# Reordering the second-level Strassen products, moving one pair of sums from GpSimd to VectorE, and storing early blocks from GpSimd

## Chip, cores, metric

One core of one Trainium2 chip. The metric is the device time of one execution in microseconds (us).

## The reference, cut to what matters

```python
# x (16, 512, 768), w1 (768, 3072), b1 (3072), w2 (3072, 768), all float32
y = np.matmul(x, w1) + b1
y = 0.5 * y * (1.0 + erf(y / np.sqrt(2.0)))
return np.matmul(y, w2)
```

## The kernel before

The 8192 rows go through in eight blocks of 1024. Each block has a *first product* (x times w1, then GELU) and a *second product* (times w2). Both use the Strassen-Winograd scheme: seven products of half-sized matrices and some sums instead of eight products. In blocks 0 and 1 the second product has one level (four *units* of 128 rows). From block 2 on it has two levels: seven outer products (here also called *units*, in the order `ORDER`), each made of seven inner products (1 to 7), each of them 12 matmuls of 192 columns, about 0.99 us. The sums that make the operands and the outputs run on VectorE, some copies on ScalarE.

Two neighbouring units are interleaved so that TensorE has something to do while sums are made:

```python
ORDER = (1, 6, 7, 5, 2, 4, 3)          # outer products, in time
# period of unit i (j is the unit before it); fill(s) records side work
p1(i); copy_xy(i)      # bX -> bY by ScalarE
p7(j)                  # adds onto bY of j: bZ must have been made from it before
fill(1); p5(i); fill(2); p3(j); fill(3)
p6(i)                  # then VectorE: bZ = bY + quarter of an earlier output
fill(4); p4(j); fill(5); p2(i); fill(6)
```

So the addition after product 6 (`bZ<-bY`) has the three products p4, p2, p1 of time, about 3 us, before product 7 of the same unit needs it done. It stands in VectorE's queue among much other work. (A *slot* is one of the six calls of `fill`; the *turn* is the stretch where the last unit of one product is interleaved with the first unit of the next.)

The seven outer products share four output buffers `par[0..3]`. Unit 5 ends a part of the sums:

```python
add, dst = {1: (None, 0), 6: (0, 1), 2: (0, 0), 7: (1, 2), 5: (None, 3),
            3: (1, 1), 4: (2, 2)}[self.p]       # which par is added, which is written
...
if self.p == 5:                                  # in finish()
    for r in range(2):                           # "row sums", VectorE
        tt(par[1][:, r], par[1][:, r], self.dst[:, r], ADD)
    for r in range(2):                           # "bottom right sums", GpSimd
        nc.gpsimd.tensor_tensor(out=self.dst[:, r], in0=par[2][:, r],
                                in1=self.dst[:, r], op=ADD)
        self.store(r)
```

Blocks 0 and 1 have one output buffer, `osb`, stored from the sync queue:

```python
def right_done(self):
    nc.sync.dma_start(out=orr[...], in_=self.o[:, 0, :])
# in the second product of blocks 0 and 1, unit 1:
load_next_x(sb + 1, range(3, 6))                 # GpSimd's queue
for n in range(4):
    load_wt((sb + 1) * NH + n)                   # for block 2: sync queue, 672 KB each
# in block 1, from slot 2 on, units 0 to 2 and once more in unit 3: one sum on VectorE and its w2s copies to DRAM
```

Of the kernel before, what the change touches and what calls it, by code (L numbers as in the profile page):

```python
# [8 lines left out]
FP32 = mybir.dt.float32  # L9
F16 = mybir.dt.float16  # L10
P = 128
ADD = mybir.AluOpType.add
# [20 lines left out]
def kernel(  # L33
# [8 lines left out]
    nc = tc.nc  # L42
# [5 lines left out]
    RH = SB // 2  # L48
    nsb = R // SB
    KQ = K // P // 2  # L50
    NH = H // P // 2
    N2 = N // 2
    NU = RH // P
# [28 lines left out]
    ONE = 2  # L82
# [10 lines left out]
    def cut(off, n, pattern=None, **dims):  # L93
        ap = arena[:, off:off + n]
        return ap.rearrange(pattern, **dims) if pattern else ap
# [4 lines left out]
           for b in range(2)]  # L100
# [2 lines left out]
        "p (r t h n) -> p r t h n", r=2, t=2, h=2) for k in range(4)]  # L103
    tmps = [cut(o_par + 3 * k * PAR, 4 * RH).bitcast(FP32).rearrange("p (a r) -> p a r", a=2)
            for k in range(2)]
    stage = [cut(o_par + k * PAR + d * WB, WB, "p (c n) -> p c n", c=NQ)
             for k in (0, 3) for d in range(2)]
    assert 14 * NH * N4 + 2 * NH * P <= o_par
# [13 lines left out]
    with tc.manual_schedule():  # L122
# [3 lines left out]
        def tt(o, a, b, op):  # L126
            nc.vector.tensor_tensor(out=o, in0=a, in1=b, op=op)  # L127

        def later(n, f, q=None):
            (queue if q is None else q).append((70 + n * 0.52, f))  # L130

        def sums(ns):

            for q in (soon, queue):
                while q and ns >= q[0][0] * 0.6:
                    ns -= q[0][0]
                    q.pop(0)[1]()

        def flush(q):
            while q:  # L140
                q.pop(0)[1]()
# [80 lines left out]
            op(3, 4, b21, t[2], None)  # L222


        ORDER = (1, 6, 7, 5, 2, 4, 3)
        w2_order = [(ORDER[0], q) for q in (1, 2, 5, 6)]
        for i in range(1, 8):
            for d, q in ((0, 1), (1, 7), (0, 5), (1, 3), (0, 6), (1, 4), (0, 2)):
# [61 lines left out]
        def half_sums(c, ks=(0, 1, 2)):  # L290

            g11, g21, g22 = G1[:, c, 0, :], G1[:, c, 1, :], G2[:, c, 1, :]
            n = len(range(NH)[c]) * RH
            for k in ks:
                o, a, b, op = ((GA[:, c, :], g21, g22, ADD), (GB[:, c, :], GA[:, c, :], g11, SUB),
                               (g21, g11, g21, SUB))[k]
                later(n, lambda o=o, a=a, b=b, op=op: tt(o, a, b, op))

        def s4_sum(r, h):

            c, rr = slice(h * NQ, (h + 1) * NQ), slice(r * 2 * P, (r + 1) * 2 * P)
            later(NQ * 2 * P, lambda: tt(GB[:, c, rr], G2[:, c, 0, rr], GB[:, c, rr], SUB))
# [4 lines left out]
        def lev_sums(i, c0=0, c1=NQ, ks=(0, 1, 2, 3), q=None):  # L307

            A = OPERAND[ORDER[i]]
            a11, a12 = A[:, c0:c1, 0:2 * P], A[:, NQ + c0:NQ + c1, 0:2 * P]  # L310
            a21, a22 = A[:, c0:c1, 2 * P:RH], A[:, NQ + c0:NQ + c1, 2 * P:RH]
            s = [t[:, c0:c1, :] for t in lev_of(i)]
            for k in ks:
                a, b, op = ((a21, a22, ADD), (s[0], a11, SUB), (a11, a21, SUB),
                            (a12, s[1], SUB))[k]
                later((c1 - c0) * 2 * P, lambda k=k, a=a, b=b, op=op: tt(s[k], a, b, op), q)


        class Unit1:
# [2 lines left out]
            C = KQ  # L322

            def __init__(self, g, sb, k):
                self.g, self.sb = g, sb
                self.hi = hi_of(sb * NH + k)
                self.wt = wts[sb * NH + k]

# [7 lines left out]
                                     stop=c == self.C - 1, skip_group_check=True)  # L336

            def alloc(self):
                self.tmp = tmps[self.g % 2]

            def c12(self):
                return self.tmp[:, 0, :]
# [14 lines left out]
        class Unit2:  # L357
# [25 lines left out]
                return self.o[:, 1, N2:N]  # L383

            def right_done(self):
                nc.sync.dma_start(out=orr[:, self.sb * 8 + self.u, :], in_=self.o[:, 0, :])

            def left_done(self, row, bank):
                nc.scalar.copy(out=self.o[:, row, 0:N2], in_=bank[:, 0:N2])
                if row == 1:  # L390
                    nc.sync.dma_start(out=orr[:, self.sb * 8 + NU + self.u, :],
                                      in_=self.o[:, 1, :])

        class Unit3:

# [6 lines left out]
            def __init__(self, g, sb, i):  # L402
                self.g, self.sb, self.i = g, sb, i
                self.p = ORDER[i]
                add, dst = {1: (None, 0), 6: (0, 1), 2: (0, 0), 7: (1, 2), 5: (None, 3),
                            3: (1, 1), 4: (2, 2)}[self.p]
                self.add = None if add is None else par[add]
                self.dst = par[dst]
                self.alloc = lambda: None
# [50 lines left out]
            def finish(self):  # L460
                if self.p in (2, 3, 4):
                    self.store(0)
                    self.store(1)
                if self.p == 5:
                    for r in range(2):
                        tt(par[1][:, r], par[1][:, r], self.dst[:, r], ADD)
                    for r in range(2):
                        nc.gpsimd.tensor_tensor(out=self.dst[:, r], in0=par[2][:, r],  # L468
                                                in1=self.dst[:, r], op=ADD)
                        self.store(r)  # L470

        def p1(u, c0, c1):
            u.mm(1, bX[u.g % 2], True, c0, c1)
# [141 lines left out]

        def fill_mm1(sb, k, slot):
            n = sb * NH + k
            if slot == 1:
                if sb < ONE:
                    if k in (5, 9):  # L620
                        for s in range(4):
                            g_sum(s, 0, k - 5, k - 1)
                    if k == NH - 1:
                        for s in range(4):
                            g_sum(s, 0, 8, 10)
                    if sb == 0 and k in (4, 6, 8, 10):
                        prep_w2(*w2_parts[(k - 4) // 2])
                elif k in (6, 10):
                    lev_sums(0, *((0, 3) if k == 6 else (3, 5)), q=soon)
                elif k >= 3 and k % 2 == 1:  # L630
                    m = (k - 3) // 2
                    half_sums(slice(m, m + NQ + 1, NQ), (0, 1, 2) if m < 4 else (0, 1))
                    if k == 9:
                        lev_sums(1, 0, 3)
                        lev_sums(2, 0, 3)
                if k + 1 < NH:
                    prep_wt(n + 1)
                sums(900)
            if slot == 4:
                sums(1500)  # L640
            if slot == 3 and sb >= ONE and sb + 1 < nsb:
                if 1 <= k < 9:
                    load_x(sb + 1, k - 1)
                if 3 <= k < 11:
                    transpose_dma(sb + 1, k - 3)
            if slot == 5:
                if k + 3 < NH and (k >= 1 or sb > 0) and n + 3 not in wts:
                    load_wt(n + 3)
                if sb == 0:
                    for part in w2_loads[:2]:  # L650
                        load_w2(*part)
                    del w2_loads[:2]
                if sb >= ONE and k >= 3:
                    for m in range(2 * (k - 3), min(2 * (k - 2), RING)):
                        load_ring(sb, m)
            if slot == 6:
                flush(soon)
                if k == NH - 1 and sb < ONE:
                    flush(queue)
# [46 lines left out]
        def fill_mm2_two(sb, k, slot):  # L706
            if k == 0:
                if slot == 1:
                    lev_sums(0, NQ - 1, NQ, (0, 1), soon)
                    flush(soon)  # L710
                    lev_sums(0, NQ - 1, NQ, (2, 3), soon)
                    half_sums(slice(NQ - 1, NQ), (0, 1))
                    lev_sums(1, 3, NQ - 1)
                if slot == 6:
                    half_sums(slice(NH - 1, NH), (0, 1))
                    lev_sums(1, NQ - 1, NQ)
                    flush(queue)
                    for m in (NQ - 2, NQ - 1):
                        half_sums(slice(m, m + NQ + 1, NQ), (2,))
                    lev_sums(2, 3, NQ)  # L720
            elif slot == 1:
                if k == 3:
                    s4_sum(1, 1)
                if k in (2, 3, 4, 5):
                    lev_sums(k + 1)
                if k == 2:
                    s4_sum(0, 1)
            if k == 1 and slot == 4:
                s4_sum(1, 0)
                s4_sum(0, 0)  # L730
            if k > 0 or slot > 1:
                sums(1200)
            if slot == 6 and k > 0:
                flush(queue)
            if sb + 1 < nsb:
                if k in (0, 5, 6) and slot == 6:
                    load_wt((sb + 1) * NH + max(k - 4, 0))
                if k == 6 and slot == 1:
                    prep_wt((sb + 1) * NH)
                    x_sums(sb + 1, queue)  # L740
# [42 lines left out]
```

## Time and profile before

| | before |
|---|---|
| median of the runs (3) | 905.48 us (901.74 to 907.42) |
| span of the profiled run | 906.2 us |
| TensorE busy | 95% |
| second product of a two-level block, blocks 2 to 6, first matmul to the next block's first | 50.45 us each |
| second product of block 1 | 56.95 us |

The top of the page of the kernel before (busy time, share of the span, number of instructions):

```profile
span 906.2 us, 16269 instructions
...
PE 860.2 (95%) x6276; PEld 560.6 (62%) x6276; DVE 666.9 (74%) x1151; ACT 417.5 (46%) x680; POOL 148.1 (16%) x194
...
```

TensorE (PE) is the engine that bounds the kernel, so its idle time is the place to look. (DVE is VectorE, ACT ScalarE, POOL GpSimd; SPq is the sync engine, which here issues DMAs. bX, bY, bZ and bW are buffers in PSUM; arena and G lie in SBUF.) The waits of TensorE, longest in total first (engine, what it wrote, its line, what released it: us in total, times, longest):

```profile
PE bY L423 <- DVE bZ L516: 13.3, 12, 1.8
PE bY L334 <- DVE bZ L521: 7.3, 7, 3.2
PE bY L372 <- ACT bY L476: 5.1, 1, 5.1
...
```

The first line is the two-level blocks: twelve waits, two in each of six blocks, for the `bZ<-bY` addition. One of each pair is 0.5 us, the other 1.8. The longer one in block 2, in TensorE's timeline (start, duration, group, count, then the idle time before it and its releaser):

```profile
355.18 1.15 PE L423 MATMUL bX<-arena 128*128 128x192 f16 x12
358.09 1.15 PE L423 MATMUL bY<-arena 128*128 128x192 f16 x12 [1.75 <-DVE bZ L516]
```

Twelve matmuls start 0.99 us after the twelve before them when nothing is in the way; here it is 2.91, so 1.92 us are lost. VectorE and GpSimd in the time before:

```profile
351.68 1.64 DVE L127 TENSOR_TENSOR arena<-arena 128x1536 f16<-128x1536 f16 x1
...
353.71 2.52 DVE L127 TENSOR_TENSOR arena<-arena 128x1536 f16<-128x1536 f16 x1
...
356.61 0.94 DVE L127 TENSOR_TENSOR arena<-arena 128x1536 f16<-128x1536 f16 x1
357.48 0.55 DVE L516 TENSOR_TENSOR bZ<-bY,arena 128x384 f32<-128x384 f32 x1
```

```profile
350.10 2.40 POOL L468 TENSOR_TENSOR arena<-arena 128x768 f32<-128x768 f32 x1 [47.32 <-DVE arena L127]
353.58 1.82 POOL L468 TENSOR_TENSOR arena<-arena 128x768 f32<-128x768 f32 x1
```

VectorE never rests here. Two operations of one and the same shape (128x1536) take 1.64 and 2.52 us, the next 0.94. The long ones are those that run beside GpSimd's two sums. The bZ addition at 357.48 stands behind them all, and TensorE behind it.

Block 1 has the other large wait. ScalarE, TensorE and the sync queue there:

```profile
231.58 0.48 ACT L389 COPY arena<-bX 128x384 f32<-128x384 f32 x1 [13.39 <-DMA out_dram<-arena]
231.95 0.49 ACT L476 COPY bY<-bX 128x384 f32<-128x384 f32 x1
```

```profile
232.49 3.79 PE L372 MATMUL bY<-arena 128*128 128x384 f16 x12 [5.07 <-ACT bY L476]
236.11 2.11 PE L372 MATMUL bY<-arena,G 128*128 128x384 f16 x12
```

```profile
219.14 0.34 SPq L386 DMA_DIRECT2D out_dram<-arena  x1
```

A store issued at 219.14 lands only at about 231.5. ScalarE's copy into that buffer waits for it for 13.4 us; the copy TensorE needs stands behind. And then twelve matmuls take 3.79 us where the next twelve take 2.11: after an idle time of 5.1 us they start at half the rate. The Trainium skill, "TensorE: Matmul & The Clock Gate", section "What's actually happening", says that the array's clock is halved after an idle window of about 3.4 us. The trace agrees on the half rate (0.320 us from matmul to matmul instead of 0.163). After the waits of 1.8 us in the two-level blocks none was slow.

### The profile page before, as it was taken

The numbers are of one execution on the slowest core, as the hardware profiler recorded it, in microseconds if no ns is written. First come the engines' busy times: TensorE is split into PE (matmuls) and PEld (weight loads), VectorE is DVE, ScalarE is ACT, GpSimd is POOL, SyncE is SP. The second block draws the span as 40 slices with busy tenths as digits, with TensorE's granted clock in tenths as the row PEclk, the third lists the DMA queues.
The fourth block names the chain that finished last, engine by engine and source line by source line (L and its number), as shares of the span: only waits on it lengthen the run. The fifth ranks groups of instructions, "written<-read, shape, count | busy, mean of one in ns | idle before, by whom it ended". The sixth has DMA issues, their size and how long they took to land.

```text
span 906.2 us, 16269 instructions
## 1 busy us (share of the span) xinstructions
PE 860.2 (95%) x6276; PEld 560.6 (62%) x6276; DVE 666.9 (74%) x1151; ACT 417.5 (46%) x680; POOL 148.1 (16%) x194
## 2 busy tenths in 40 slices
PE   6989999989799999999999999999999999999995
PEld 2434654446454499546984479644996469844795
DVE  3688665645456699558995699767996689947995
ACT  2665116750147721576117751377215762177520
POOL 5553002400000003210041001300032000300013
PEclk8999999999999999999999999999999999999998
DMA  9999989949969789997999969997899969966495
GB/s 154 119 187 152 208 288 202 225 110 289 334 176 247 221 283 315 274 302 178 305 346 242 301 202 297 311 273 217 277 306 286 291 186 317 341 206 223 147 291 213
DMA packets 176525, 222.96 MB, mean 246 GB/s; under 512 B 106944, under 2 KB 115904, under 8 KB 176448
## 3 DMA queue, kind: packets, MB, share of 16 engines
q1 hardware_dynamic: 111680, 176.31, 62.2%
q0 software_dynamic: 64768, 45.62, 29.3%
q8 instruction: 49, 0.80, 0.3%
q14 instruction: 28, 0.23, 0.1%
HBM read 189.74 MB, written 47.87 MB: 262 GB/s over the span
## 4 chain that ended last, share of the span: by engine, by line
PE 67%; DVE 14%; DMA 10%; issue 4%; POOL 2%; ACT 2%; SPq 0%; POOLq 0%; DVEq 0%; ACTq 0%
PE bY L334 17%; PE bX L334 11%; PE bY L423 8%; DVE arena L127 7%; PE bW L334 5%; PE bZ L334 5%; PE bY L372 5%; PE bX L423 5%; DMA wt<-in_w_dram 4%; DMA wt<-w1s 4%; PE bX L372 3%; PE bW L423 3%; PE bZ L423 3%; DMA out_dram<-arena 1%; PE bZ L372 1%
## 5 line engine op out<-in xcount | busy, mean ns | idle before, releaser
L334 PEld LDWEIGHTS <-wt 128*128 128x128 f16 x2016 | 197.1, 98 | 250.9 <-issue 19.6
L423 PEld LDWEIGHTS <-arena 128*128 128x128 f16 x2664 | 221.2, 98 | 20.8 <-issue 15.1
L483 DVE TENSOR_TENSOR arena<-bY,pw 128x512 f32<-128x512 f32 (+1 forms) x104 | 70.8, 680 | 153.9 <-PE bY L334 98.7
L334 PE MATMUL bY<-XT,wt 128*128 128x512 f16 x576 | 155.8, 379 | 7.5 <-DVE bZ L521 7.3
L334 PE MATMUL bX<-XT,wt 128*128 128x512 f16 x576 | 143.0, 381 | 1.6 <-DMA wt<-w1s 1.5
L476 ACT COPY bY<-bX 128x512 f32<-128x512 f32 (+1 forms) x146 | 80.4, 551 | 131.9 <-DVE arena L455 105.0
L349 ACT ACTIVATE G<-arena,b1t 128x1024 f16<-128x1024 f32 x96 | 110.3, 1149 | 64.3 <-DVE arena L506 64.3
L127 DVE TENSOR_TENSOR arena<-arena 128x1536 f16<-128x1536 f16 (+5 forms) x176 | 129.7, 758 | 10.7 <-DMA w2s<-arena 9.8
L423 PE MATMUL bY<-arena 128*128 128x192 f16 x1224 | 115.6, 246 | 13.3 <-DVE bZ L516 13.3
L493 ACT COPY pw<-bW 128x512 f32<-128x512 f32 (+1 forms) x146 | 80.8, 554 | 83.0 <-PE bW L423 44.6
L334 PE MATMUL bW<-XS,wt 128*128 128x512 f16 x288 | 78.7, 383 | 4.0 <-DVE wt L127 4.0
L506 DVE TENSOR_TENSOR arena<-bZ,pw 128x512 f32<-128x512 f32 (+1 forms) x104 | 70.4, 677 | 15.9 <-PE bZ L334 14.0
L334 PE MATMUL bY<-XS,wt 128*128 128x512 f16 x288 | 79.1, 384 | 1.0 <-DVE wt L127 0.4
L468 POOL TENSOR_TENSOR arena<-arena 128x768 f32<-128x768 f32 x12 | 25.3, 2107 | 328.6 <-DVE arena L127 242.8
L334 PE MATMUL bZ<-XS,wt 128*128 128x512 f16 x288 | 78.5, 382 | 0.0
L248 POOL DMA_DIRECT2D xh<-in_x_dram x56 | 30.1, 542 | 283.8 <-DMA XT<-xh 280.6
L423 PEld LDWEIGHTS <-G 128*128 128x128 f16 x864 | 72.5, 98 | 4.8 <-issue 1.9
L354 ACT ACTIVATE G<-bX,b1t 128x512 f16<-128x512 f32 x96 | 65.4, 681 | 10.4 <-PE bX L334 10.4
L354 ACT ACTIVATE G<-bY,b1t 128x512 f16<-128x512 f32 x96 | 64.7, 674 | 0.0
L127 DVE TENSOR_TENSOR arena<-arena,G 128x1024 f16<-128x1024 f16 (+4 forms) x98 | 59.8, 610 | 1.7
L127 DVE TENSOR_TENSOR arena<-G 128x768 f16<-128x768 f16 (+3 forms) x98 | 59.3, 605 | 0.0
L372 PEld LDWEIGHTS <-arena 128*128 128x128 f16 x384 | 38.1, 99 | 31.5 <-issue 7.0
(51 smaller groups left out, 868.9 us busy)
## 6 DMA issues: line engine op xcount, KB each, us to landing
arena<-w2s SPq DMA_DIRECT2D x294, 288.0 KB, 4.1
wt<-w1s SPq DMA_DIRECT2D x72, 672.0 KB, 6.7
out_dram<-arena POOLq DMA_DIRECT2D x48, 384.0 KB, 5.5
w2s<-arena SPq DMA_DIRECT2D x49, 288.0 KB, 4.4
xh<-in_x_dram POOLq DMA_DIRECT2D x56, 192.0 KB, 6.9
wt<-in_w_dram POOLq DMA_DIRECT2D x48, 192.0 KB, 6.7
w1s<-wt SPq DMA_DIRECT2D x12, 672.0 KB, 4.4
out_dram<-arena SPq DMA_DIRECT2D x16, 384.0 KB, 3.8
```

The lines of the kernel that those rows point to most:

```text
L127: nc.vector.tensor_tensor(out=o, in0=a, in1=b, op=op)
L248: nc.gpsimd.dma_start(out=xh, in_=xr[:, sb * 8 + t, :])
L334: nc.tensor.matmul(out=dst[:, 0:RH], lhsT=self.wt[:, slot, c, :], rhs=a[:, c, :], start=first and c == 0, stop=c == self.C - 1, skip_group ...
L349: nc.scalar.activation(out=G2[:, hi, :, :], in_=self.tmp, func=GELU, bias=b1t[:, NH + hi:NH + hi + 1])
L354: nc.scalar.activation(out=G1[:, hi, row, :], in_=bank[:, 0:RH], func=GELU, bias=b1t[:, hi:hi + 1])
L372: nc.tensor.matmul(out=dst[:, 0:N2], lhsT=a, rhs=w2o[:, slot, :, c, :], start=first and c == 0, stop=c == self.C - 1, skip_group_check=True)
L423: nc.tensor.matmul(out=dst[:, t * N4:(t + 1) * N4], lhsT=a, rhs=w[:, c, :], start=first and c == 0 and t == 0, stop=c == NQ - 1, skip_grou ...
L468: nc.gpsimd.tensor_tensor(out=self.dst[:, r], in0=par[2][:, r], in1=self.dst[:, r], op=ADD)
L476: nc.scalar.copy(out=bY[u.g % 2][:, 0:u.F], in_=bX[u.g % 2][:, 0:u.F])
L483: nc.vector.tensor_tensor(out=u.c22(), in0=bY[u.g % 2][:, 0:u.F], in1=w[:, 0:u.F], op=ADD)
L493: nc.scalar.copy(out=w[:, 0:u.F], in_=bW[:, 0:u.F])
L506: nc.vector.tensor_tensor(out=u.c12(), in0=bZ[:, 0:u.F], in1=w[:, 0:u.F], op=ADD)
```

## The change

Its intent: take the bottom right sums from GpSimd and give them to VectorE at a time when it has room, namely in the next block's first product; arrange outer products and side sums so that VectorE is never late for a bZ addition; and take the stores of the early blocks out of the crowded sync queue. The diff, cut to its core:

```diff
+    tmps0 = [cut(o_lev + ...) ...]            # temporaries of the first product that leave par[3] alone
-        ORDER = (1, 6, 7, 5, 2, 4, 3)
+        ORDER = (1, 6, 2, 7, 5, 4, 3)
 # Unit1
-                self.tmp = tmps[self.g % 2]
+                self.tmp = (tmps0 if self.sb > ONE and self.k < 4 else tmps)[self.g % 2]
 # Unit2: stores of blocks 0 and 1
-                nc.sync.dma_start(out=orr[:, self.sb * 8 + self.u, :], in_=self.o[:, 0, :])
+                nc.gpsimd.dma_start(out=orr[:, self.sb * 8 + self.u, :], in_=self.o[:, 0, :])
 # Unit3
-                            3: (1, 1), 4: (2, 2)}[self.p]
+                            3: (1, 1), 4: (2, 0)}[self.p]
                 if self.p == 5:
                     for r in range(2):
-                        tt(par[1][:, r], par[1][:, r], self.dst[:, r], ADD)
-                    for r in range(2):
-                        nc.gpsimd.tensor_tensor(out=self.dst[:, r], in0=par[2][:, r], ...)
-                        self.store(r)
+                        later(2 * N2, lambda r=r: tt(par[1][:, r], par[1][:, r], par[3][:, r], ADD), soon)
+            def c22_sum(self, r):
+                tt(par[3][:, r], par[2][:, r], par[3][:, r], ADD)
+                self.store(r)
 # first product of the next block, first two units
+            if sb > ONE and k in (0, 1) and slot == 2:
+                units3[5].c22_sum(k)
 # second product: level sums of the third unit before the in-place half sums,
 # s4_sum(1,1) and s4_sum(0,1) from the third and fourth to the fifth unit (cut)
```

Level sums, half sums and s4 sums are sums on VectorE that make operands of the second product. Product 4 used to be written over `par[2]`. Now `par[2]` is still wanted when product 4 is made, because the bottom right sum comes later. So product 4 goes to `par[0]`.

More of the change, by code (lines that the diff above doesn't have):

```diff
@@ L105 @@
             for k in range(2)]
+    tmps0 = [cut(o_lev + 4 * k * RH, 4 * RH).bitcast(FP32).rearrange(
+        "p (a r) -> p a r", a=2) for k in range(2)]
     stage = [cut(o_par + k * PAR + d * WB, WB, "p (c n) -> p c n", c=NQ)
@@ L324, in __init__ @@
             def __init__(self, g, sb, k):
-                self.g, self.sb = g, sb
+                self.g, self.sb, self.k = g, sb, k
                 self.hi = hi_of(sb * NH + k)
@@ L390, in left_done @@
                 if row == 1:
-                    nc.sync.dma_start(out=orr[:, self.sb * 8 + NU + self.u, :],
-                                      in_=self.o[:, 1, :])
+                    nc.gpsimd.dma_start(out=orr[:, self.sb * 8 + NU + self.u, :],
+                                        in_=self.o[:, 1, :])
+        units3 = {}
         class Unit3:
@@ L404, in __init__ @@
                 self.p = ORDER[i]
+                units3[self.p] = self
                 add, dst = {1: (None, 0), 6: (0, 1), 2: (0, 0), 7: (1, 2), 5: (None, 3),
-                            3: (1, 1), 4: (2, 2)}[self.p]
+                            3: (1, 1), 4: (2, 0)}[self.p]
                 self.add = None if add is None else par[add]
@@ L465, in finish @@
                     for r in range(2):
-                        tt(par[1][:, r], par[1][:, r], self.dst[:, r], ADD)
-                    for r in range(2):
-                        nc.gpsimd.tensor_tensor(out=self.dst[:, r], in0=par[2][:, r],
-                                                in1=self.dst[:, r], op=ADD)
-                        self.store(r)
+                        later(2 * N2, lambda r=r: tt(par[1][:, r], par[1][:, r], par[3][:, r],
+                                                     ADD), soon)
+            def c22_sum(self, r):
+                tt(par[3][:, r], par[2][:, r], par[3][:, r], ADD)
+                self.store(r)
         def p1(u, c0, c1):
@@ L714, in fill_mm2_two @@
                 if slot == 6:
+                    flush(queue)
                     half_sums(slice(NH - 1, NH), (0, 1))
@@ L717, in fill_mm2_two @@
                     flush(queue)
+                    lev_sums(2, 3, NQ)
                     for m in (NQ - 2, NQ - 1):
                         half_sums(slice(m, m + NQ + 1, NQ), (2,))
-                    lev_sums(2, 3, NQ)
             elif slot == 1:
-                if k == 3:
-                    s4_sum(1, 1)
                 if k in (2, 3, 4, 5):
                     lev_sums(k + 1)
-                if k == 2:
+                if k == 4:
+                    s4_sum(1, 1)
                     s4_sum(0, 1)
@@ L730, in fill_mm2_two @@
                 s4_sum(0, 0)
-            if k > 0 or slot > 1:
+            if k == 1 and slot < 4:
+                sums(300)
+            elif k > 0 or slot > 1:
                 sums(1200)
@@ L734, in fill_mm2_two @@
                 flush(queue)
+            if k == 6:
+                if slot == 1:
+                    flush(soon)
+                if sb + 1 == nsb and slot in (4, 5):
+                    units3[5].c22_sum(slot - 4)
             if sb + 1 < nsb:
```

## The prediction

> **What bounds it.** TensorE: the page has it busy 95% of 906.2 us. In the timeline its matmuls start every 0.216 us (512 columns), 0.163 (384), 0.082 (192); gaps beyond that sum to 52 us.
>
> **Where the change can act.**
> (a) Each of the six two-level blocks has about 3.0 us of gaps: 0.2-0.3 at the turn, 0.15 to 0.24 before product 4 of the first unit, 0.63 before product 7 of the second, 1.92 before product 7 of the sixth. The view of waits lays the last two to VectorE's bZ addition (13.3 us, 12 waits). Cause of the 1.92: VectorE is nearly saturated (busy 49.7 of 52 us in 317-369), and while GpSimd does its two bottom right sums (2.40 and 1.82 us, from 350.1) two VectorE 128x1536 subtractions take 1.64 and 2.52 instead of 0.95. This is the exclusive shared port of the Trainium skill, "SBUF — State Buffer", "Who interferes with whom"; the trace agrees.
> (b) In block 1 TensorE waits 5.1 us at 227 for ScalarE's bY copy, which stands behind a copy waiting 13.4 us for an output store on the sync queue (12.3 us to land); then 12 matmuls run at half rate, 1.8 us more.
>
> **What the change does.** No matmul is added. 12 GpSimd sums go; 12 VectorE ones come (0.95 each) in the next block's first product, where VectorE has room. With product 2 third, the in-place half sum (2 x 0.68) moves behind the bZ addition; row sums (2 x 0.95) and s4 sums move later.
>
> Adding up VectorE's new queue with traced spacings (0.87 for 1536, 0.47 for PSUM forms and 768, 0.60 for 2x512) from 323.05:
> - second unit's bZ addition ends at 327.0, needed at 327.7: the 0.63 goes, and nearly all of the 0.15;
> - third unit's ends about 334.9, needed at 334.6: a new gap of about 0.4;
> - sixth unit's ends 1.2 us ahead: the 1.92 goes.
> Gain about 2.3 us a block: 14 us (12 to 16).
>
> Early stores: issued earlier (219.1 to 217.5, 224.0 to 218.5), but in GpSimd's queue behind three x loads that took from 218 to 227 to move. The skill's "DMA: Bandwidth & Descriptors", "Queues, rings and completion order", has each DMA engine drain a ring in order and alternate between queues; so the first store lands about 230 instead of 231.5. Most of the 5.1 us stays; the next unit's stores, behind two more x loads, may be 1 us late. Gain 1 us (-1 to +6).
>
> Tail: six stores bunch in the last 6 us; at about 350 KB/us that is just absorbed: 0 to 1 us lost.
>
> **Prediction.** 905.5 - 14 - 1 + 0.5 = 891 us, 8 in 10 within 886 to 897. Faster by over 2% (under 887.4): 0.2; within 2%: 0.79; slower by over 2%: 0.01.
>
> **What would show each step.** GpSimd has no additions; all 128x1536 VectorE operations take about 0.95. The waits of bY for bZ's addition fall from 13.3 to about 2.5 us, at the third unit. Block 1's wait for the bY copy is still 3 to 5 us. The last matmul ends about 14 us earlier.
>
> **What would make it wrong.** Block 1's wait vanishes entirely (about 885); the third unit's gap is 1 us or more, or level sums come late for a product (895 or above); ring loads (0.92 DMA share in the second product) become what TensorE waits for.

## The result, and the profile after

| | before | after |
|---|---|---|
| median of 4 runs | 905.57 us | 892.02 us (891.38 to 896.39) |
| ratio, 95% interval | | 0.9869 (0.983 to 0.9908) |
| span of the profiled run | 906.2 us | 894.6 us |
| second product, blocks 2 to 6 | 50.45 us each | 48.29 us each |
| second product, block 1 | 56.95 us | 62.21 us |
| last matmul starts | 898.0 us | 886.7 us |

A ratio is the mean time of one kernel's fast runs over that of the other's fast runs of the same rounds, so it is not quite the ratio of the medians quoted. (The record lists a fifth run of the changed kernel, 894.40 us, that the median leaves out.)

```profile
span 894.6 us, 16259 instructions
...
PE 859.8 (96%) x6276; PEld 560.6 (63%) x6276; DVE 663.9 (74%) x1163; ACT 418.2 (47%) x680; POOL 131.2 (15%) x198
...
```

VectorE has 12 instructions more (1163 against 1151) and is nevertheless busy 3 us less. As predicted, GpSimd has no addition left, and none of the 152 VectorE operations of 128x1536 takes more than 0.96 us. The waits of TensorE (line numbers have moved: L423 is now L428, L516 is L522, L476 is L482, L127 is L129):

```profile
...
PE bY L374 <- DVE arena L129: 3.8, 1, 3.8
...
PE bY L374 <- ACT bY L482: 3.4, 1, 3.4
PE bY L428 <- DVE bZ L522: 2.1, 6, 0.3
```

The 13.3 us in twelve waits have become 2.1 us in six: one short one in each two-level block. It is the predicted one, at the third unit. VectorE's bZ addition and TensorE there:

```profile
334.48 0.95 DVE L129 TENSOR_TENSOR arena<-G 128x1536 f16<-128x1536 f16 x1
335.35 0.56 DVE L522 TENSOR_TENSOR bZ<-bY,arena 128x384 f32<-128x384 f32 x1
```

```profile
333.47 2.14 PE L428 MATMUL bX<-arena,G 128*128 128x192 f16 x24
335.96 1.15 PE L428 MATMUL bY<-arena 128*128 128x192 f16 x12 [0.35 <-DVE bZ L522]
```

Twenty-four matmuls need 1.98 us start to start; it was 2.49, so 0.51 us are lost. At the sixth unit, where 1.92 us were lost before, nothing is:

```profile
355.18 0.56 DVE L522 TENSOR_TENSOR bZ<-bY,arena 128x384 f32<-128x384 f32 x1
355.65 2.69 DVE L129 TENSOR_TENSOR arena<-arena 128x1536 f16<-128x1536 f16 x3
```

```profile
355.76 1.15 PE L428 MATMUL bX<-arena 128*128 128x192 f16 x12
356.75 1.15 PE L428 MATMUL bY<-arena 128*128 128x192 f16 x12
```

The bZ addition ends at 355.74, 1.0 us before product 7 starts.

The early blocks are another story. In block 1 the one stall has become two:

```profile
226.85 0.48 ACT L391 COPY arena<-bX 128x384 f32<-128x384 f32 x1 [12.12 <-DMA out_dram<-arena]
...
245.77 0.48 ACT L391 COPY arena<-bX 128x384 f32<-128x384 f32 x1 [11.75 <-DMA out_dram<-arena]
```

```profile
226.97 0.76 DVE L129 TENSOR_TENSOR arena<-arena 128x1152 f16<-128x1152 f16 x1 [11.85 <-DMA w2s<-arena]
```

```profile
227.76 3.03 PE L374 MATMUL bY<-arena 128*128 128x384 f16 x12 [3.79 <-DVE arena L129]
...
246.68 4.00 PE L374 MATMUL bY<-arena 128*128 128x384 f16 x12 [3.43 <-ACT bY L482]
```

```profile
213.90 0.55 POOL L388 DMA_DIRECT2D out_dram<-arena  x1
...
236.30 1.15 POOL L250 DMA_DIRECT2D xh<-in_x_dram  x2 [20.72 <-DMA XT<-xh]
237.45 0.55 POOL L388 DMA_DIRECT2D out_dram<-arena  x1
```

The first store is now issued at 213.90, but the copy that waits for it still waits for 12.1 us. The second one is issued at 237.45 because it stands in GpSimd's queue behind two x loads that wait for transposes. The view says that the first stall ended with the w2s copy VectorE waited for; ScalarE's copy at 226.85 and that one came within 0.1 us of each other, so either would have held TensorE.

Where the 11.6 us of the profiled run went, by the start of each block's products: block 0, -0.6; first product of block 1, -2.9; its second product, +5.3; then, with small steps either way in the first products, six second products of -2.1 to -2.2 each, -12.9 in all. The first product of block 1 must not be read as an effect: it took 60.8 to 65.5 us in the profiles of all kernels, in no order that fits their edits. The traces show where the difference lies: VectorE, and TensorE behind it, wait there for the landing of a w1 load (`wt<-in_w_dram`). Its longest wait is 4.0 us in the profile with 65.5 us (the kernel before), 2.9 in the changed kernel's with 62.6, and at most 1.3 in the six profiles under 62 us. Why the load lands late in some of them is not shown. So a span of a single profile is worth no more than about 3 us, and I compare stages.

### The profile page after: what moved, and what is told of

Read it like the earlier page. It is cut to its first block, busy times and chain, and to the rows that moved or that the text cites. A ratio compares the mean times of both kernels' runs of the same rounds, so it can differ in the third digit from the quotient of the medians.

```text
span 894.6 us, 16259 instructions
## 1 busy us (share of the span) xinstructions
PE 859.8 (96%) x6276; PEld 560.6 (63%) x6276; DVE 663.9 (74%) x1163; ACT 418.2 (47%) x680; POOL 131.2 (15%) x198
## 4 chain that ended last, share of the span: by engine, by line
PE 65%; DMA 14%; DVE 14%; issue 4%; POOL 1%; ACT 1%; SPq 1%; DVEq 0%; POOLq 0%; ACTq 0%
PE bY L336 16%; PE bX L336 10%; PE bY L428 9%; DVE arena L129 7%; PE bW L336 5%; PE bX L428 5%; PE bZ L336 5%; PE bY L374 4%; DMA wt<-in_w_dram 4%; PE bZ L428 3%; DMA XT<-xh 3%; PE bW L428 3%; PE bX L374 3%; DMA wt<-w1s 2%; DMA xh<-in_x_dram 2%
## 5 line engine op out<-in xcount | busy, mean ns | idle before, releaser
L428 PEld LDWEIGHTS <-arena 128*128 128x128 f16 x2664 | 221.2, 98 | 8.7 <-issue 3.0
L351 ACT ACTIVATE G<-arena,b1t 128x1024 f16<-128x1024 f32 x96 | 110.5, 1151 | 62.6 <-DVE arena L512 62.6
L129 DVE TENSOR_TENSOR arena<-arena 128x1536 f16<-128x1536 f16 (+5 forms) x188 | 127.6, 702 | 14.5 <-DMA w2s<-arena 13.8
L482 ACT COPY bY<-bX 128x512 f32<-128x512 f32 (+1 forms) x146 | 80.5, 551 | 120.0 <-DVE arena L460 90.2
L428 PE MATMUL bY<-arena 128*128 128x192 f16 x1224 | 115.7, 246 | 2.1 <-DVE bZ L522 2.1
L452 POOL DMA_DIRECT2D out_dram<-arena x48 | 34.5, 720 | 416.3 <-DVE arena L510 361.5
L428 PEld LDWEIGHTS <-G 128*128 128x128 f16 x864 | 72.5, 98 | 4.0 <-issue 1.2
L356 ACT ACTIVATE G<-bX,b1t 128x512 f16<-128x512 f32 x96 | 65.5, 682 | 9.1 <-PE bX L336 9.1
L129 DVE TENSOR_TENSOR arena<-arena,G 128x1024 f16<-128x1024 f16 (+4 forms) x98 | 60.0, 612 | 2.0
L129 DVE TENSOR_TENSOR arena<-G 128x768 f16<-128x768 f16 (+3 forms) x98 | 59.5, 607 | 0.0
```

The source lines that it names most:

```text
L129: nc.vector.tensor_tensor(out=o, in0=a, in1=b, op=op)
L351: nc.scalar.activation(out=G2[:, hi, :, :], in_=self.tmp, func=GELU, bias=b1t[:, NH + hi:NH + hi + 1])
L356: nc.scalar.activation(out=G1[:, hi, row, :], in_=bank[:, 0:RH], func=GELU, bias=b1t[:, hi:hi + 1])
L428: nc.tensor.matmul(out=dst[:, t * N4:(t + 1) * N4], lhsT=a, rhs=w[:, c, :], start=first and c == 0 and t == 0, stop=c == NQ - 1, skip_grou ...
L452: nc.gpsimd.dma_start(out=orr[:, s0:s0 + 2, right * N2:(right + 1) * N2], in_=self.dst[:, r].rearrange("p t h n -> p t (h n)"))
L482: nc.scalar.copy(out=bY[u.g % 2][:, 0:u.F], in_=bX[u.g % 2][:, 0:u.F])
```

## The experiments

Ten kernels were run, each correct unless said otherwise. Times are medians; those of one group shared a chip and the runs of the kernel before. *Second product* is that of a two-level block in the profile, alike within 0.02 us in blocks 2 to 6 unless said otherwise.

| kernel | median us | ratio to before (95%) | second product |
|---|---|---|---|
| before (first group, 11 runs) | 905.27 | | 50.45 |
| changed, again | 894.45 | 0.9877 (0.9856 to 0.9898) | 48.27 |
| changed, early stores on sync | 893.89 | 0.9884 (0.9858 to 0.991) | 48.27 |
| changed, block 2's weights late | 887.88 | 0.9799 (0.9775 to 0.9824) | 48.27 |
| changed, bottom right sums on GpSimd | 895.72 | 0.9894 (0.987 to 0.9918) | 48.27, and 0.9 at the turn |
| before (second group, 11 runs) | 904.95 | | |
| before, without bottom right sums (wrong) | 892.79 | 0.9872 (0.9846 to 0.9897) | 48.55 |
| before, with deferred VectorE sums | 938.34 | 1.0371 (1.0348 to 1.0394) | 56 to 57 |
| late weights and one s4 sum later | 884.83 | 0.9788 (0.9765 to 0.9811) | 47.77 |
| the same, early stores on sync | 889.55 | 0.9839 (0.9817 to 0.9862) | 47.78 |
| before (third group, 7 runs) | 904.90 | | |
| before, VectorE sums in GpSimd's place | 901.41 | 0.9961 (0.9924 to 0.9998) | 49.93 |
| changed, VectorE sums in that place | 896.09 | 0.9893 (0.9848 to 0.9938) | 48.63, and 0.7 at the turn |

### The changed kernel again

No edit.

> The changed kernel again, unaltered, as the yardstick for the runs beside it. Expected 890 to 894 us, ratio to before 0.984 to 0.988; again about 0.8 us of TensorE gaps in each two-level block (0.29 or 0.19 + 0.10 at the turn, 0.51 before product 7 of the third unit). Open: whether block 1's second product again takes 62 us, as in the first profile (before: 57).

Measured: 894.45 us, a little above the expected band, ratio 0.9877 inside it. The gaps were the same ones (0.28 at the turn of block 2, 0.51 at the third unit). Block 1's second product took 59.7 us, again with two stalls (2.8 and 3.8 us): the two stalls are no accident of the first profile.

### Is it the port? The sums left out

```diff
-                        nc.gpsimd.tensor_tensor(out=self.dst[:, r], in0=par[2][:, r],
-                                                in1=self.dst[:, r], op=ADD)
                         self.store(r)          # the kernel before; result wrong on purpose
```

> The kernel before, with the GpSimd bottom right sums left out and the unsummed block stored (a wrong result on purpose); VectorE's program is untouched. Theory P (shared port): the two 128x1536 VectorE operations of 1.64 and 2.52 us go back to 0.95, and the 1.92 us TensorE wait before product 7 of the sixth unit goes wholly (VectorE is then 2.3 us earlier there), while the 0.63 and the 0.15 to 0.24 stay: second products of 48.5 us instead of 50.45, 10 to 12 us faster than before over six blocks. Rival L (VectorE is merely short of time at the burst of row sums): the wait stays at 1.5 us or more and the time within 3 us of before.

Measured: 892.79 us, 12 us faster than before, second products of 48.55 us. VectorE's program is the same to the instruction, and its operations beside the former sums:

```profile
350.41 0.94 DVE L127 TENSOR_TENSOR arena<-arena 128x1536 f16<-128x1536 f16 x1
...
351.75 0.94 DVE L127 TENSOR_TENSOR arena<-arena 128x1536 f16<-128x1536 f16 x1
```

1.64 and 2.52 have become 0.94. Of TensorE's twelve waits (13.3 us) for the bZ addition six are left (its line is L514 here):

```profile
...
PE bY L423 <- DVE bZ L514: 2.8, 6, 0.5
```

The 1.92 us wait is gone, the 0.63 stays. So GpSimd's 12 sums cost TensorE 1.9 us a block by slowing VectorE alone. This is what the Trainium skill, "SBUF — State Buffer", section "Who interferes with whom", describes: a VectorE instruction with two SBUF inputs and a GpSimd instruction that reads SBUF exclude each other.

### Is it the port? The sums put back

```diff
+            def row_sum(self, r):              # the changed kernel, at the place of the row sums
+                tt(par[1][:, r], par[1][:, r], par[3][:, r], ADD)
+                nc.gpsimd.tensor_tensor(out=par[3][:, r], in0=par[2][:, r], in1=par[3][:, r], op=ADD)
+                self.store(r)
-                units3[5].c22_sum(k)           # both places taken out
```

> The changed kernel with the bottom right sums back on GpSimd, each right behind its row sum; order and stores stay as changed. Theory P (shared port): while GpSimd sums, the VectorE 128x1536 sums for the next block's x take 1.6 to 2.5 us instead of 0.95, VectorE loses about 2.3 us there, and a new TensorE wait of 0.8 to 2 us per block comes before product 7 of the last unit or at the turn in blocks 2 to 6: 5 to 9 us slower than the changed kernel. Rival L (VectorE is only short of time, GpSimd costs it nothing): VectorE has 12 operations fewer, so no new wait and the same time within 1 us.

Measured: a new loss of 0.9 us (a wait of 0.7) in each of blocks 2 to 6, before product 7 of the last unit at the turn, as theory P said. But the kernel is only 1.3 us slower than the changed one (895.72 against 894.45), not 5 to 9. I had counted on two slowed VectorE operations; only one was:

```profile
353.69 2.40 POOL L475 TENSOR_TENSOR arena<-arena 128x768 f32<-128x768 f32 x1 [13.08 <-DVE arena L129]
357.14 1.82 POOL L475 TENSOR_TENSOR arena<-arena 128x768 f32<-128x768 f32 x1
```

```profile
354.33 0.55 DVE L460 TENSOR_TENSOR arena<-bX,arena 128x384 f32<-128x384 f32 x1
354.80 0.54 DVE L492 TENSOR_TENSOR arena<-bY,pw 128x384 f32<-128x384 f32 x1
...
357.33 2.46 DVE L129 TENSOR_TENSOR XS<-XS,XT 128x1536 f16<-128x1536 f16 x1
```

The first sum ran beside operations that take one input from PSUM (bX, bY): 0.55 and 0.54, unharmed, as the same section of the skill says of instructions with at most one SBUF input. Only at its start was there an operation with both inputs in SBUF, a row sum that had begun 0.2 us earlier: that one kept its 0.95, and GpSimd's sum took 2.40 instead of 1.82. The second sum met one with both inputs in SBUF that began after it, and this took 2.46 instead of 0.95. So the one that came second waited, whichever engine it was. The five losses make 4.5 us. That only 1.3 are seen comes, in the two profiles, mostly from a first product of block 1 that is 1.7 us shorter, which the edit does not touch, and from a tail (the time after the last matmul's start) that is 0.7 us shorter.

### VectorE's sums in GpSimd's old place

```diff
-                        nc.gpsimd.tensor_tensor(out=self.dst[:, r], in0=par[2][:, r], ...)
+                        tt(self.dst[:, r], par[2][:, r], self.dst[:, r], ADD)   # the kernel before
```

> The kernel before, with the bottom right sums given to VectorE in the place where GpSimd had them, right behind the row sums; no delay into the next block, old order, early stores on the sync queue. VectorE then pays 2 x 0.87 us for them in front of the sixth unit's bZ addition, where the shared port had cost it 2.3. So the 1.92 us wait shrinks to about 1.4, the others stay: second products of 49.9 us, about 3 us faster than before. If the place did not matter, it would go wholly (48.5).

Measured: second products of 49.93 us, 901.41 us, as expected. The loss before product 7 of the sixth unit is 1.04 us with another 0.35 just before it, 1.4 together. Changing the engine alone is worth 0.5 us a block.

### The deferred VectorE sums in the old order

The kernel before with `c22_sum`, `tmps0` and the calls in the next block's first product, and:

```diff
-                            3: (1, 1), 4: (2, 2)}[self.p]
+                            3: (1, 1), 4: (2, 0)}[self.p]      # ORDER stays 1,6,7,5,2,4,3
```

> The kernel before, with only the bottom right sums moved to VectorE in the next block's first product: old order 1,6,7,5,2,4,3, early stores on the sync queue. If the 1.92 us wait comes from the GpSimd sums and the rest from the order, the 1.92 goes and the 0.63 and 0.15 to 0.24 stay: second products of 48.5 us, 10 to 12 us faster than before. The order itself is then worth only 0.25 us a block (0.63 + 0.15 less the new 0.51), about 1.5 us in all. Rival (the order is what frees VectorE): the 1.92 stays at 1 us or more. Possible extra: product 4's output reuses a buffer whose store has just been issued, which may add a wait of its own.

This was the surprise: 938.34 us, 33 us *slower* than before. The 1.92 us wait did go, and the 0.63 stayed. But what I had put down as a "possible extra" is the largest number. Waits of TensorE, and VectorE at the place:

```profile
PE bY L428 <- DVE arena L486: 32.4, 7, 6.8
...
```

```profile
355.73 0.56 DVE L460 TENSOR_TENSOR arena<-bX,arena 128x384 f32<-128x384 f32 x1 [2.72 <-DMA out_dram<-arena]
361.49 0.56 DVE L486 TENSOR_TENSOR arena<-bY,pw 128x384 f32<-128x384 f32 x1 [5.20 <-DMA out_dram<-arena]
```

Product 4 writes to `par[0]`, and in the old order product 2 comes just before it: its stores have just been issued (350.64 and 353.31 in the trace), and VectorE waits for them to land. The second takes 8.1 us to land, beside three weight loads of 672 KB that were issued just before it. TensorE loses about 6 us, and some matmuls at half rate, in blocks 2 to 6. In the new order two units (7 and 5) lie between product 2 and product 4, two periods of 6.9 us more, and no such wait appears in the profile of the changed kernel. So the order is not a fine adjustment of VectorE's load worth 0.25 us a block: with these four buffers it is what lets the sums be deferred without that wait. No run tried another buffer for product 4, or the new order without the moved side sums.

### The changed kernel with the sums not deferred

```diff
+                    for r in range(2):
+                        later(2 * N2, lambda r=r: self.c22_sum(r), soon)   # behind the row sums
-                units3[5].c22_sum(k)                                       # both places taken out
```

> The changed kernel with the bottom right sums on VectorE, but right behind the row sums instead of in the next block's first product. In the changed kernel the last unit's bZ addition ends 0.6 us ahead of need; 1.6 us more of VectorE work in front of it gives a new TensorE wait of about 1 us at the turn in blocks 2 to 6: 4 to 6 us slower than the changed kernel. If VectorE had room there, the same time within 1 us.

Measured: the profile shows what was expected, 0.35 us before product 4 and 0.71 before product 7 of the last unit, 1.06 a block in blocks 2 to 6. The timed runs show 896.09 us, ratio 0.9893 with an interval of 0.9848 to 0.9938: slower than the changed kernel's 0.9877 by an amount that the interval does not settle. Deferring is worth 1.06 us a block by the profile; the whole time was expected 4 to 6 us longer and that is not shown. (In this profile, too, the tail is 0.7 us shorter than the changed kernel's, 7.08 against 7.83.)

### Early stores back on the sync queue

```diff
-                nc.gpsimd.dma_start(out=orr[:, self.sb * 8 + self.u, :], in_=self.o[:, 0, :])
+                nc.sync.dma_start(out=orr[:, self.sb * 8 + self.u, :], in_=self.o[:, 0, :])
                 # and the other row likewise
```

> The changed kernel with only the early stores put back on the sync queue. Theory A (the DMA engines are full in block 1 and the x loads stand ahead in GpSimd's queue, so the queue of the stores matters little): within 2 us of the changed kernel, block 1's second product 55 to 59 us with one stall of about 5 us. Rival (the GpSimd stores are worth 3 us or more in the timed runs, and the first profile was an exception): 3 to 7 us slower than the changed kernel. The two-level blocks are as in the changed kernel, 48.3 us of second product each.

Measured: 893.89 against 894.45 us, no difference; block 1's second product 58.3 us with one stall of 5.5 us. Theory A stands: as the change has them, the early stores on GpSimd's queue gain nothing in all.

The profiles show that this nothing is the sum of two differences. With block 2's weights early, block 1's second product took 57.0 to 58.3 us in the five profiles with the stores on the sync queue, and 58.5 to 62.2 in the four with GpSimd's: about 2 us in favour of the sync queue, though each is a single profile. The tail is the reverse: 9.57 us here against 7.83, although the last store landed earlier (6.01 us after the last matmul's start against 6.43). What ends later is a closing instruction of GpSimd, a DRAIN (8.8 us after that start against 6.8); why it depends on the queue of stores so much earlier is not shown.

### The weight loads of block 2 later

```diff
-                for n in range(4):
-                    load_wt((sb + 1) * NH + n)
+                if sb == 0:
+                    for n in range(4):
+                        load_wt((sb + 1) * NH + n)
+            if sb == 1 and (k, slot) in ((2, 6), (3, 4)):
+                for n in ((0, 1) if k == 2 else (2, 3)):
+                    load_wt((sb + 1) * NH + n)
```

> The changed kernel with the four weight loads of block 2 (672 KB each) issued at the third and fourth unit of block 1's second product instead of all four at the second. Theory A1 (these 2.7 MB fill the DMA engines in front of the w2s stores and beside the output stores, and that causes block 1's stalls): the stalls of about 4 + 3.6 us and the cold matmuls after them mostly go, block 1's second product takes 53 to 57 us instead of 62, and the kernel is 5 to 9 us faster than the changed one. Rival A2 (the x loads ahead in GpSimd's queue alone hold the stores): under 2 us of gain, the stalls stay over 3 us each.

Measured: 887.88 us, 6.6 us faster than the changed kernel; block 1's second product 52.5 us, both stalls gone. Theory A1 stands: with the four loads of 672 KB out of the middle of the w2s copies, the first store of the block landed after 7.8 us instead of 12.9, and what TensorE had waited for was there in time. Which copies and stores had stood behind the loads, and which beside them, was not separated. One wait of 2.3 us came instead, for the first of these weights at the turn to block 2: they were now a little too late.

```profile
247.28 0.94 PE L336 MATMUL bX<-XT,wt 128*128 128x512 f16 x3 [2.26 <-DMA wt<-w1s]
248.02 3.72 PE L374 MATMUL bY<-arena 128*128 128x384 f16 x12
```

The twelve matmuls behind it again run at half rate (3.72 us instead of 2.11), after a wait of only 2.26 us.

### Both repairs, and the queue of the early stores again

The late weights one step earlier for the first two, and one s4 sum out of the third unit's way:

```diff
+            if sb == 1:
+                for n in {(2, 5): (0,), (2, 6): (1,), (3, 4): (2, 3)}.get((k, slot), ()):
+                    load_wt((sb + 1) * NH + n)
             elif slot == 1:
+                if k == 3:
+                    s4_sum(1, 0)
             if k == 1 and slot == 4:
-                s4_sum(1, 0)
                 s4_sum(0, 0)
```

> The changed kernel with the weight loads of block 2 late (the first two one step earlier than in the run with late weights, to be rid of its 2.3 us wait for the first weights) and with one of the two s4 sums (0.87 us) moved from the second unit's slots to the fourth's. The 0.51 us wait of the third unit goes (its bZ addition ends about 0.4 us ahead of need), no new wait in the later units: second products of 47.8 us. Block 1's second product about 50 to 51 us. Together 882 to 885 us, 2 to 5 us faster than with late weights alone, 9 to 12 faster than the changed kernel.

Measured: 884.83 us (882.61 to 887.84), 2.1% faster than before and 9.6 us faster than the changed kernel's repetition (which was in another group). Second products take 47.77 us: the 0.51 us wait is gone and no other came. Block 1's second product takes 50.05 us, and at the turn to block 2, just behind it, three short gaps cost 1.4 us. In the waits of TensorE nothing is left of the two-level second products:

```profile
PE bT L261 <- DMA G<-in_x_dram: 5.4, 5, 2.8
PE bW L336 <- DVE wt L129: 4.0, 1, 4.0
PE bY L336 <- DVE bZ L527: 3.4, 7, 0.6
PE bX L336 <- DMA wt<-w1s: 2.6, 2, 1.4
...
```

The first two are the start of the kernel; the third and fourth belong to the first products. This is the version to keep.

The same with the early stores on the sync queue:

> The same with the early stores on the sync queue instead of GpSimd's. If GpSimd's queue matters once the weight loads are out of the way, this one is 2 to 5 us slower in block 1 (stores behind the w2s copies and transposes on the sync queue); if the weight loads were all that mattered, both are within 1.5 us of each other.

Measured: 889.55 us, 4.7 us slower. Here the queue does matter. The profile shows a stall of 4.4 us at the turn, where the last products of block 1 run between the first of block 2, with matmuls at half rate after it: the last store is issued on the sync queue at 242.48, straight behind two of the weight loads, and VectorE can write to the buffer only at 254.03:

```profile
241.43 0.96 SPq L159 DMA_DIRECT2D wt<-w1s  x2
242.48 1.75 SPq L393 DMA_DIRECT2D out_dram<-arena  x1
```

```profile
254.03 0.56 DVE L489 TENSOR_TENSOR arena<-bY,pw 128x384 f32<-128x384 f32 x1 [7.19 <-DMA out_dram<-arena]
```

The store took 11.4 us to land, and both loads landed before it. In the other kernel the same store, issued on GpSimd's queue at 240.95 just behind the same loads, took 7.5 us and landed before them: on that queue it shares the DMA engines with the loads instead of standing behind them. That fits the Trainium skill, "DMA: Bandwidth & Descriptors", section "Queues, rings and completion order" (each DMA engine alternates between queues and drains each in order). The two kernels differ in nothing but the queue of these stores; so with the loads late it was worth 4.7 us, and with the loads early nothing. Not all of the 4.7 is this stall: in the profiles 1.7 us are again the longer tail (9.56 us against 7.84).

## Why the prediction was right

The time was predicted as 891 us and came out as 892.02, by a sum whose largest term was right (14 us predicted, 12.9 measured) and whose small ones were partly luck.

- *Two-level blocks, 14 us (12 to 16):* measured 12.9 us over six blocks. "The 0.63 goes, and nearly all of the 0.15": they did; 0.10 stays in every other block. "The 1.92 goes": it did, and the addition ended 1.0 us ahead where 1.2 was reckoned. "A new gap of about 0.4" at the third unit: 0.51. The waits were to fall from 13.3 to about 2.5 us; they fell to 2.1.
- *The port as the cause:* right, and shown three ways: without the sums the slow operations are fast and the wait is gone (48.55 against 50.45 us); on VectorE in the same place the loss is 1.4; with GpSimd back, a loss of 0.9 returns where an operation with two SBUF inputs meets a sum. The step from engine to saving needs the place too: of the 2.2 us that a block gained, the change of engine alone gave 0.5.
- *"With product 2 third, the in-place half sum moves behind the bZ addition":* true, and too small a reason. What the order is for, the buffer of product 4, the prediction did not see. With the old order the deferred sums cost 33 us.
- *Early stores, 1 us (-1 to +6):* no difference in the timed runs (894.45 us against 893.89 with the stores on the sync queue). "The first store lands about 230 instead of 231.5": the copy that waits for it waited 12.1 us instead of 13.4, about the gain foreseen (its clock time, 226.85, is that of a block that began 3.5 us earlier). "Block 1's wait for the bY copy is still 3 to 5 us" was right about that wait (3.4), but I expected one stall and there were two, of 4.0 and 3.6 us, each followed by matmuls at half rate: the "1 us late" of the next unit's stores was too little. In the profiles that made block 1 about 2 us slower than with the stores on the sync queue. That no time was lost is luck: the shorter tail gave 1.7 us back, and the prediction did not have that.
- *Tail, 0 to 1 us lost:* the time from the last matmul's start to the end went from 8.19 to 7.88 us; nothing was lost. In the run that left the early stores on the sync queue it was 9.57; so this term came out right because the stores were moved, which the prediction did not reckon with.
- *"The last matmul ends about 14 us earlier":* in the profile the last one starts 11.3 us earlier; the rest is block 1.
- *Not settled:* why a w1 load lands late in the first product of block 1 in some profiles and not in others (up to 4.7 us), and why GpSimd's closing instruction ends later when the early stores are on the sync queue.

## What to carry to other kernels

GpSimd work on SBUF is not free because GpSimd is idle: look at the durations of one and the same VectorE shape, and where they double beside a GpSimd operation, the cost is VectorE's. When work is deferred, ask what buffer it keeps alive and who is next to write there; the time to wait for is the landing of a store, not its issue, and a change of order may be there for that alone. And when a store lands late, look first for large prefetches that were issued with it and are not yet needed: moving them gained more (6.6 us) than moving the store to another queue (nothing), and only after that did the queue matter (4.7 us, of which 1.7 lie in the tail).

## What the Trainium skill lacked or had wrong

- "DMA: Bandwidth & Descriptors", "Issuing engines are not separate DMA queues": it says that issuing from several engines will only save the time it takes to initiate the DMAs. In these runs the same stores on another engine's queue gave 884.83 against 889.55 us; in part, since a store behind two 672 KB loads in one queue took 11.4 us to land, and on the other queue, issued just behind the same loads, 7.5 us. The page's own section "Queues, rings and completion order" explains it; that sentence leaves it out.
- "SBUF — State Buffer", "Who interferes with whom": right in all that these runs show, but it gives no duration for a VectorE operation with two SBUF inputs that meets a sum. Here 128x1536 f16 operations of 0.95 us took 1.64, 2.52 and 2.46; an estimate from the traces, what was left of the sum when they began plus 0.95, makes 1.77, 2.64 and 2.58, so nearly the whole of the rest was waited for.
- "DMA: Bandwidth & Descriptors", "Anatomy of one DMA": its fit of 2.0 us plus the bytes at 436 GB/s gives 2.9 us for a store of 384 KB (an estimate from the page). On GpSimd's queue, the path that the fit is for, the shortest landing of such a store seen here took 2.6 us, the median in the kernel before 5.5, and the longest in block 1 of the changed kernel 13.0. The fit is for one DMA by itself; what a kernel waits for is the landing among the others.
- "TensorE: Matmul & The Clock Gate", "What's actually happening": the half rate is there, but the idle window of about 3.4 us is not what these runs show. Matmuls were slow after waits of 2.00 (in two kernels), 2.26, 2.38 and 2.59 us; after one of 2.24 and one of 3.24 us, and after all those from 1.2 to 1.93 us, they were not.
